# A PEER step on one core: the norms' rows loaded for each use, their memory a place for fetched rows in between

## The chip, the cores and the metric

The kernel runs on one core of a Trainium2 chip. The metric is the device time of one execution in microseconds (us). The engines are named as in the profile: PE (TensorE, matmuls; PEld its weight loads), DVE (VectorE), ACT (ScalarE), POOL (GpSimd) and SP (SyncE, which only issues DMAs here). Each runs its own instructions in the order in which the scheduler wrote them, and waits for the others by semaphores.

## The reference, cut to what matters

One decoder layer on 512 prompt tokens and 32 sample tokens: a mixer (retention heads and a causal convolution on a shared projection), a layer norm, a retrieval of experts (PEER), a second layer norm.

```python
def layer_norm(x, g, b): ...  # over 1024 features, then * g + b
...
x = layer_norm(ALPHA * x + mix, ln1_g, ln1_b)
ffn = peer(x, w_query, sub_keys_1, sub_keys_2, peer_u, peer_v)
x = layer_norm(ALPHA * x + ffn, ln2_g, ln2_b)

def peer(...):            # per token and head (8 heads)
    s1, s2 = q1 @ keys1, q2 @ keys2      # 128 scores each
    v1, i1 = top_k(s1, 16); v2, i2 = top_k(s2, 16)
    sv, ci = top_k(v1[:, None] + v2[None, :], 16)
    idx = e1 * 128 + e2                  # one of 16384 experts
    gate = softmax(sv)
    act = gelu(peer_u[idx] . x)
    out = sum(gate * act * peer_v[idx])  # 128 experts a token
```

## The kernel before

**Two ways to the experts.** For 288 of the token rows the experts are fetched. A *slot* is one expert for each of 128 partitions: an indirect DMA on POOL's queue (`gather`, L670) brings 128 rows of `uv` (a u row and a v row of 1024 numbers each, 1 MB a slot) into a *place*, a tile named `g`; DVE takes the dot of the u half with the token (L676, the *dot*), ACT the gelu and the gate (L687, L688), and DVE adds the weighted v half to the accumulator (L693, the *sum*). The place is then free. Three gathers follow one another: the first 128 prompt tokens (I, 128 slots, numbers 0 to 127), the samples (Is, 32 slots, four heads' groups side by side on the partitions), the next 128 prompt tokens (Ib, 128 slots). The other 256 tokens go the dense way: all 128 x 128 experts are scored on PE (`scores_of`, L947, one *key* of 128 experts at a time, a 512 KB load by SP), and the chosen ones are picked by one-hot products (`build`: A, M and B on DVE and ACT, L1076 on PE), whose result is multiplied into the gelus (Ga to Gd, L1092 and L1105 on DVE); then the products with the v rows (L1133).

**The stages, in the order of the program.** The front: the first 128 tokens alone up to their expert numbers I0, then the mixer for all the others (convolution, rope, retention, output product, first norm). It has its own pools, among them `gx`, one place. Then the selection of the dense tokens' experts (`retrieve`, a long row of top-16 steps on DVE), with 44 keys' scores on PE beside it (`early_keys`); a turn of the numbers and gates into columns (L986 to L1007, with transposes L995 and ACT's copies, L999 to L1003, among them e2T); the *first pass* (`first_keys`: one-hot products for 96 keys and the scores of the 52 that are left of them); and last the products with the v rows, the second pass for the last 32 keys, and the gather Ib beside them (`phases` and `fetched`).

**Places.** `gp` has three. In the front every fourth slot up to 47 (`KX`) goes to `gx`, so there are four; the front's memory then goes to other pools, and slots 48 to 127 have the three of `gp`. Samples have three up to slot 30 and then a fourth, `gx2`, when the first pass is over; Ib has four, and five from slot 60.

**The norms' rows.** `ln1` (two tiles `lng`, `lnb` of 128 x 1024, the gain and offset on every partition) is loaded on POOL's queue behind the first rope and used by `mix_norm` up to the last chunk of the front (its last norm, tile `states`). `ln2` is loaded over the same two tiles by ACT's queue, and used by `finish` and at the end.

**What sets the order.** The scheduler of the framework lays out each engine's rows by priority, in the order in which the program emits them, as soon as its own timeline lets them start. `hold(k, ins)` puts the dots from slot k on behind an instruction of the mixer on DVE; `fence` does so for the later gathers.

## Time and profile before

| | us |
|---|---|
| runs shown | 1483.18, 1489.50, 1489.53 (median 1489.5) |
| profiled execution | 1488.64 |
| its span | 1486.7 |
| first fetch issued | 118.8 |
| last dot of I / of Is / of Ib | 743 / 909 / 1458 |

A row of the table of stretches gives the stretch, its length, and for each engine the busy time and the instructions, then the granted clock of PE, the mean busy share of the 16 DMA engines and their GB/s. With one source line asked for, the busy time is that line's alone. A row of the timeline has start and duration, engine, line, operation, and in brackets the idle time before it and what ended it. A matmul of 32-bit numbers is recorded twice, so a key's scores are 16 records and a v row's products 8.

### The profile page before, as it was taken

What the parts mean: (1) busy time and instruction counts of PE and PEld (TensorE: products, weight loads), DVE (VectorE), ACT (ScalarE), POOL (GpSimd) and SP (SyncE); (2) the same over time, 40 slices, a digit from 0 to 9 for tenths busy, and PEclk for the clock granted to TensorE, in tenths of its full rate; (3) what the DMA queues carried; (4) which work ended last, traced back from release to release, by engine and by line L of the source; (5) the groups of instructions that cost most, each with busy time, mean ns of one, the idle gap of its engine ahead of it and who ended that gap; (6) DMA issues with size and microseconds to landing.
All of it is one profiled execution on the core that took longest, in us unless ns stands there. A gap on an engine that the chain in (4) does not pass through costs nothing.

```text
span 1486.7 us, 19633 instructions
## 1 busy us (share of the span) xinstructions
PE 1415.3 (95%) x6666; PEld 966.0 (65%) x6666; DVE 1168.2 (79%) x2874; ACT 498.8 (34%) x1496; POOL 426.3 (29%) x397
## 2 busy tenths in 40 slices
PE   8899889999999999989999998998999999999998
PEld 7878455568767588878877873433454666666443
DVE  5829957998759999988878999777989766666666
ACT  1424753354122222245445534113673111111110
POOL 2171213334232221333222231243333322222230
PEclk9889899999999999999999999998999999999999
DMA  9749568978987789999988996999999999999995
GB/s 347 299 171 364 203 229 310 387 290 308 356 329 300 257 335 346 346 375 345 340 309 333 343 336 231 368 424 384 359 369 392 413 402 410 413 406 409 407 409 196
DMA packets 99537, 503.63 MB, mean 339 GB/s; under 512 B 10183, under 2 KB 21191, under 8 KB 56549
## 3 DMA queue, kind: packets, MB, share of 16 engines
q0 software_dynamic: 42240, 305.12, 52.6%
q1 hardware_dynamic: 52157, 190.10, 33.8%
q10 hardware_dynamic: 5040, 7.16, 1.5%
q8 instruction: 52, 0.85, 0.2%
q14 instruction: 48, 0.39, 0.1%
HBM read 496.97 MB, written 5.80 MB: 338 GB/s over the span
## 4 chain that ended last, share of the span: by engine, by line
PE 46%; DVE 23%; DMA 17%; issue 7%; ACT 4%; POOL 2%; ACTq 0%; SPq 0%; DVEq 0%; POOLq 0%
PE pB L1133 22%; PE sp L947 13%; DMA g<-in_uv_dram,I 7%; PE mm L217 7%; DVE acc L693 6%; DVE g L676 5%; DMA g<-in_uv_dram,Ib 5%; DMA g<-in_uv_dram,Is 4%; ACT blk L283 2%; PE mm L1076 1%; PE mm L532 1%; POOL g L670 1%; DVE iu L575 1%; PE mm L899 1%; DVE B L1060 1%
## 5 line engine op out<-in xcount | busy, mean ns | idle before, releaser
L947 PE MATMUL sp<-x1T,uv 128*128 128x256 f32 x2048 | 467.7, 384 | 2.0 <-ACT Gc L1091 1.0
L693 DVE SCALAR_TENSOR_TENSOR acc<-g,wgt,acc 128x1024 f32<-128x1024 f32 x285 | 365.1, 1281 | 86.9 <-ACT wgt L688 85.3
L947 PEld LDWEIGHTS sp<-x1T,uv 128*128 128x128 f32 x2048 | 385.7, 191 | 68.6 <-issue 13.9
L676 DVE SCALAR_TENSOR_TENSOR g<-g,x 128x1024 f32<-128x1024 f32 x288 | 350.7, 1219 | 94.2 <-DMA g<-in_uv_dram,Ib 39.9
L670 POOL DMA_INDIRECT g<-in_uv_dram,I x128 | 166.4, 1300 | 438.5 <-DVE acc L693 209.0
L670 POOL DMA_INDIRECT g<-in_uv_dram,Ib x128 | 159.3, 1245 | 360.8 <-PE pB L1133 128.7
L687 ACT ACTIVATE act<-act 128x1 f32<-128x1 f32 x288 | 57.9, 202 | 591.0 <-DVE g L676 577.0
L1133 PE MATMUL pB<-uv,Ga 128*128 128x512 f32 x352 | 158.3, 596 | 0.0
L217 PE MATMUL mm<-x1T,w 128*128 128x384 f32 (+1 forms) x448 | 152.5, 498 | 0.0
L217 PEld LDWEIGHTS mm<-x1T,w 128*128 128x128 f32 x448 | 84.4, 190 | 62.9 <-issue 30.8
L1133 PE MATMUL pB<-uv,Gb 128*128 128x512 f32 x256 | 115.1, 602 | 5.8 <-DMA uv<-in_uv_dram 4.1
L1133 PEld LDWEIGHTS pB<-uv,Ga 128*128 128x128 f32 x352 | 65.7, 190 | 69.5 <-issue 66.5
L1133 PE MATMUL pB<-uv,Gd 128*128 128x512 f32 x256 | 110.0, 592 | 0.0
L1133 PEld LDWEIGHTS pB<-uv,Gb 128*128 128x128 f32 x256 | 47.5, 190 | 70.2 <-issue 52.7
L1133 PEld LDWEIGHTS pB<-uv,Gd 128*128 128x128 f32 x256 | 48.6, 190 | 60.8 <-issue 59.3
L1052 ACT ACTIVATE off<-row,e1T 128x128 bf16<-128x128 bf16 x256 | 78.7, 392 | 2.0 <-PE mm L1076 1.8
L670 POOL DMA_INDIRECT g<-in_uv_dram,Is x32 | 41.5, 1296 | 123.0 <-DVE Ga L1105 36.9
L1133 PE MATMUL pB<-uv,Gc 128*128 128x512 f32 x160 | 75.9, 620 | 0.1
L1076 PEld LDWEIGHTS <-A 128*128 128x128 f16 x1024 | 45.5, 98 | 44.7 <-issue 28.2
L1089 ACT ACTIVATE W<-sp 128x256 f32<-128x256 f32 (+26 forms) x84 | 26.7, 318 | 133.9 <-PE sp L947 109.0
L217 PE MATMUL mm<-g,w 128*128 128x160 f32 (+1 forms) x512 | 67.0, 291 | 1.1 <-ACT score L589 1.1
L1076 PE MATMUL mm<-B,A 128*128 128x96 f16 (+1 forms) x1024 | 49.5, 192 | 18.7 <-DVE Ga L1105 7.4
(309 smaller groups left out, 1613.6 us busy)
## 6 DMA issues: line engine op xcount, KB each, us to landing
uv<-in_ut_dram SPq DMA_DIRECT2D x128, 512.0 KB
uv<-in_uv_dram SPq DMA_DIRECT2D x128, 512.0 KB
w<-in_w_in_dram SPq DMA_DIRECT2D x18, 1024.0 KB
w<-in_w_query_dram SPq DMA_DIRECT2D x15, 1024.0 KB
w<-in_w_out_dram SPq DMA_DIRECT2D x7, 1024.0 KB
g<-in_uv_dram,I POOLq DMA_INDIRECT x128, 8.3
g<-in_uv_dram,Ib POOLq DMA_INDIRECT x128, 9.4
x1T<-in_xT_dram ACTq DMA_DIRECT2D x1, 1536.0 KB
```

The source lines that it names most:

```text
L217: T.matmul(p[:, :n], w[m // 2][:, k, (m % 2) * 128:(m % 2 + 1) * 128], xT[:, k, c0:c0 + n], start=(k == 0), stop=(k == 7))
L283: S.activation(rows[j * 32:j * 32 + 32, g], u_p[g * 32:g * 32 + 32, m, p0 + j:p0 + j + w], AF.Copy)
L532: last = T.matmul(banks_[q][:, s * 256:(s + 1) * 256], src[:, k, c0:c0 + C], wo[q * 2 + s][:, k0 + k, :], start=(xT is None and k0 == 4 an ...
L670: fetch = G.indirect_dma_start(out=t, out_offset=None, in_=a["uv"], in_offset=bass.IndirectOffsetOnAxis(ap=idx[:, k:k + 1], axis=0))
L676: dot = V.scalar_tensor_tensor(t[:, :D], t[:, :D], 1.0, x1, op0=OP.mult, op1=OP.mult, accum_out=act[:, 0:1])
L687: S.activation(act[:, 1:2], act[:, 0:1], AF.Gelu)
L693: V.scalar_tensor_tensor(acc, v, wgt, acc, op0=OP.mult, op1=OP.add)
L947: mm = T.matmul(sp[:, i], u[:, k], x1T[:, k, NG2:], start=(k == 0), stop=(k == 7), skip_group_check=True)
L1052: S.activation(off[:, t], row, AF.Abs, bias=e1T[:, t1 + t:t1 + t + 1])
L1076: mm = T.matmul(pt[:, t % nt], A[t % TB], B[:, q, t % TB // 2, :, t % 2], start=(q == 0), stop=(q == 1))
L1089: S.activation(W[:, :n], sp[:, :n], AF.Gelu)
L1133: return [T.matmul(pB[b][q], W[:, b * 128:(b + 1) * 128], vt[:, q * 512:(q + 1) * 512], start=False, stop=(e == NK - 1), skip_group_check= ...
```

## The change

The rows of the norms become one tile `ln` of 128 x 2048, the size of a place, in the pool `per` with one buffer (`shared`). `norm_rows` loads both halves on POOL's queue: ln1 before the first norm as before, ln1 once more before the other chunks' norms, ln2 before the first `finish`, and ln2 once more before the samples' `finish`. In between, slots of the gather take the same tile. The gather's first 40 slots (`K5`) are emitted ahead of the rest of the front, with a priority 1100 later, and have five places (three of `gp`, `gx`, `ln`); slots 40 to 47 have four as before; 48 to 55 the three of `gp`; 56 to 119 four (`gp` and `ln`); 120 to 127 three. The samples have four up to slot 25 and three up to 29. The numbers of `hold` grow by three or four.

```diff
+K5 = 40
+K4 = (56, 120)
...
+    ln = []
+
+    def shared():
+        return per.tile([128, 2 * D], F32, name="ln")
+
+    def norm_rows(which, after=None):
+
+        t = shared()
+        ln[:] = [t[:, 0:D], t[:, D:]]
+        for half, part in zip(ln, "gb"):
+            src = a[f"{which}_{part}"]
+            load = nc.gpsimd.dma_start(half, bass.AP(tensor=src.tensor, offset=src.offset, ap=[[0, 128], [1, D]]))
+            if after is not None:
+                await_(load, after)
...
-        layer_norm(x1, n, ln1[0], ln1[1], src)
+        layer_norm(x1, n, ln[0], ln[1], src)
...
-                pool = gx if k < KX and k % 4 == 3 else gp
+                pools = (gp, gp, gp, gx, per) if k < K5 else (gp, gp, gp, gx) if k < KX else (gp, gp, gp, per)
+                if KX <= k < K4[0] or k >= K4[1]:
+                    pools = (gp,)
...
-                pool = gp if k < FREE else (gp, gp, gp, gx2[0])[k % 4]
-            t = pool.tile([128, 2 * D], F32, name="g")
+                pools = (gp, gp, gp, per) if k < FREE - 4 else (gp,) if k < FREE else (gp, gp, gp, gx2[0])
+            pool = pools[k % len(pools)]
+            t = shared() if pool is per else pool.tile([128, 2 * D], F32, name="g")
...
-    ln1 = [bc_row("lng", a["ln1_g"], D, q=nc.gpsimd, after=lastq), bc_row("lnb", a["ln1_b"], D, q=nc.gpsimd, after=lastq)]
+    norm_rows("ln1", lastq)
...
     conv_s(yS, normed)
+    now = tc.cur_priority
+    tc.cur_priority = now + 1100
+    gather0 = gather(x1_0, I0, g0_gates, acc0, range(PH * TK))
+    for _ in range(K5):
+        next(gather0)
+    tc.cur_priority = now
...
-    hold(44, conv_norm(y, n))
+    hold(48, conv_norm(y, n))
...
+    norm_rows("ln1")
     gate_heads(ons[1], gT, NS)
...
-    gather0 = gather(x1_0, I0, g0_gates, acc0, range(PH * TK))
-    for _ in range(KX):
+    for _ in range(KX - K5):
         next(gather0)
...
-    ln2 = [bc_row("lng", a["ln2_g"], D), bc_row("lnb", a["ln2_b"], D)]
...
+        norm_rows("ln2")
         finish(x1_0, [acc0[:, 0:512], acc0[:, 512:]], 128, [(0, 128, o[0][0, 0:128])], room())
...
+        norm_rows("ln2")
         t = room()
```

The dots and sums that stand on DVE ahead of some rows, counted in the order:

| ahead of | before: dots, sums | now |
|---|---|---|
| the last chunk of the first tokens' numbers (I0) | 12, 8 | 13, 9 |
| the first rope of the other tokens (L230) | 24, 23 | 26, 25 |
| the last norm of the front (L514, states) | 55, 54 | 58, 57 |
| the first top-16 step of the selection | 67, 65 | 69, 68 |
| the second table of expert numbers (L992) | 107, 105 | 116, 115 |
| the first product into Ga (L1105) | 112, 110 | 119, 117 |
| the last product of the first pass into Ga | 158, 156 | 158, 156 |

The lines of the changed kernel are higher by 17 to 27 (L670, L676, L693 are now L690, L696, L713; L992 is L1017, L1005 L1030, L1105 L1130, L1092 L1117).

DVE at the turn into columns, from the second table of expert numbers (L992, tile e) to the cast of the gates (L1005, gtT), before:

```order
L992 TENSOR_SCALAR e_4242<-e_4242 128x128
L1056 TENSOR_TENSOR M<-iot,e2T 128x768
L693 SCALAR_TENSOR_TENSOR acc<-g,wgt,acc 128x1024
L1060 TENSOR_TENSOR B<-M,gtT 128x768 x2
L676 SCALAR_TENSOR_TENSOR g,act<-g,x_0_129 128x1024
L1056 TENSOR_TENSOR M<-iot,e2T 128x768
L693 SCALAR_TENSOR_TENSOR acc<-g,wgt,acc 128x1024
L676 SCALAR_TENSOR_TENSOR g,act<-g,x_0_129 128x1024
L693 SCALAR_TENSOR_TENSOR acc<-g,wgt,acc 128x1024
L676 SCALAR_TENSOR_TENSOR g,act<-g,x_0_129 128x1024
L693 SCALAR_TENSOR_TENSOR acc<-g,wgt,acc 128x1024
L1005 CAST gtT<-e_4249 128x128
```

The same place now (L1017 to L1030):

```order
L1017 TENSOR_SCALAR e_4240<-e_4240 128x128
L650 TENSOR_REDUCE Es<-oh 128x32
L696 SCALAR_TENSOR_TENSOR g,act<-g,x_0_129 128x1024
L1037 CAST Is<-Es 128x32
L713 SCALAR_TENSOR_TENSOR acc<-g,wgt,acc 128x1024
L1030 CAST gtT<-e_4247 128x128
```

Three dots and four sums stood between the two rows, and now one of each. On PE, behind the transposes of that table, two more keys' scores stood ahead of the first one-hot products, and now one.

DVE near the end of the first pass, from the first product that takes 13 keys of Gc on (Ga, Gb and Gc are the dense block's gates times gelus), before:

```order
L1105 SCALAR_TENSOR_TENSOR Gc<-mm,Gc 128x13x4
L693 SCALAR_TENSOR_TENSOR acc<-g,wgt,acc 128x1024
L1105 SCALAR_TENSOR_TENSOR Ga<-mm,Ga 128x44x4
L1092 TENSOR_TENSOR Gc<-Gc,W 128x224
L1056 TENSOR_TENSOR M<-iot,e2T 128x768
L1105 SCALAR_TENSOR_TENSOR Ga<-mm,Ga 128x44x4
L1092 TENSOR_TENSOR Gc<-Gc,W 128x228
L676 SCALAR_TENSOR_TENSOR g,act<-g,x_0_7032 128x1024
L1105 SCALAR_TENSOR_TENSOR Gb<-mm,Gb 128x32x4
L1105 SCALAR_TENSOR_TENSOR Gc<-mm,Gc 128x14x4
L1060 TENSOR_TENSOR B<-M,gtT 128x768 x2
L676 SCALAR_TENSOR_TENSOR g,act<-g,x_0_7032 128x1024
```

and now:

```order
L1130 SCALAR_TENSOR_TENSOR Gc<-mm,Gc 128x13x4
L696 SCALAR_TENSOR_TENSOR g,act<-g,x_0_7033 128x1024
L1130 SCALAR_TENSOR_TENSOR Gb<-mm,Gb 128x32x4
L1130 SCALAR_TENSOR_TENSOR Gc<-mm,Gc 128x14x4
L1085 TENSOR_TENSOR B<-M,gtT 128x768 x2
L1130 SCALAR_TENSOR_TENSOR Ga<-mm,Ga 128x44x4
L1117 TENSOR_TENSOR Gc<-Gc,W 128x228
L713 SCALAR_TENSOR_TENSOR acc<-g,wgt,acc 128x1024
L1130 SCALAR_TENSOR_TENSOR Ga<-mm,Ga 128x44x4
L1117 TENSOR_TENSOR Gc<-Gc,W 128x232
```

From that row to the last product into Ga there were six dots, two of them in these rows, and now there is one.

POOL at the second load of ln1, which is now between fetches (I is the table of slot rows; hrs is the scale of a retention chunk's head norm):

```order
L690 DMA ln<-in_uv_dram,I_133 128x2048
L690 DMA g<-in_uv_dram,I_133 128x2048 x4
L184 DMA ln<-in_ln_g_dram 128x1024
L184 DMA ln<-in_ln_b_dram 128x1024
L212 TENSOR_SCALAR hrs<-hrs 128x4
L213 TENSOR_TENSOR hrs<-hrs,mhalf 128x4
L690 DMA g<-in_uv_dram,I_133 128x2048 x4
```

The first row is slot 39, the last one in `ln`; the loads wait for its sum on DVE, and the head norm's scale and slots 44 to 47 stand behind them.

More of the change, by code (lines that the diff above doesn't have):

```diff
@@ L660, in gather @@
             if x1 is x1_0:
-                pool = gx if k < KX and k % 4 == 3 else gp
+                pools = (gp, gp, gp, gx, per) if k < K5 else (gp, gp, gp, gx) if k < KX else (gp, gp, gp, per)
+                if KX <= k < K4[0] or k >= K4[1]:
+                    pools = (gp,)
             elif late:
-                pool = (gp, gp, gp, gx2[0])[k % 4] if k < 60 else (gp, gp, gp, gx2[0], bx)[k % 5]
+                pools = (gp, gp, gp, gx2[0]) if k < 60 else (gp, gp, gp, gx2[0], bx)
             else:
-                pool = gp if k < FREE else (gp, gp, gp, gx2[0])[k % 4]
-            t = pool.tile([128, 2 * D], F32, name="g")
+                pools = (gp, gp, gp, per) if k < FREE - 4 else (gp,) if k < FREE else (gp, gp, gp, gx2[0])
+            pool = pools[k % len(pools)]
+            t = shared() if pool is per else pool.tile([128, 2 * D], F32, name="g")
             at = step(k) if late else -1
@@ L700, in finish @@
             V.scalar_tensor_tensor(t[:n, c], x1[:n, c], ALPHA, f[h][:n], op0=OP.mult, op1=OP.add)
-        layer_norm(t, n, ln2[0], ln2[1], table=table)
+        layer_norm(t, n, ln[0], ln[1], table=table)
         for p0, p1, dst in dsts:
@@ L858, in tile_step @@
     retain(2, *before(2))
-    hold(45, steps["p"])
+    hold(49, steps["p"])
     banks[:] = [ps]
@@ L880, in tile_step @@
     retain(3, *third)
-    hold(47, steps["p"])
+    hold(51, steps["p"])
     gate_heads(ons[2], gT, NS + C)
@@ L885, in tile_step @@
     mix_b(NS, C)
-    hold(49, steps["ln"])
+    hold(53, steps["ln"])
     xrs[0], pms[0] = fe.tile([128, D], F32, name="xr0"), None
@@ L893, in tile_step @@
     mix_b(NS + C, C)
-    hold(53, steps["ln"])
+    hold(56, steps["ln"])
     pq0, known = [mmps() for _ in range(4)], NS + 2 * C
@@ L904, in tile_step @@
     mix_b(NS + 2 * C, C, parts[1])
-    hold(55, steps["ln"])
+    hold(58, steps["ln"])
     for m in range(4):
@@ L1227, in tile_step @@
         t = gp.tile([128, 2 * D], F32, name="g")[:, :D]
-        layer_norm(t, 128, ln2[0], ln2[1], pB[b], True)
+        layer_norm(t, 128, ln[0], ln[1], pB[b], True)
         for q in range(2):
```

## The prediction

> **What bounds the kernel now.** I read the page first, for its span and the slices.
>
> ```profile
> span 1486.7 us, 19633 instructions
> PE 1415.3 (95%) x6666; PEld 966.0 (65%) x6666; DVE 1168.2 (79%) x2874; ACT 498.8 (34%) x1496; POOL 426.3 (29%) x397
> ...
> DVE  5829957998759999988878999777989766666666
> ...
> DMA  9749568978987789999988996999999999999995
> ```
>
> VectorE (DVE) is full only in the middle, the DMA engines from slice 25 on. The 79% and 95% average over stages with different limits, so the second view is the table of stretches, cut at the front, the prompt block's waits, the dense block's selection, its conversion to one-hot rows, the first pass over the keys, and the rest.
>
> ```profile
> core 0: us, PE busy (x) PEld busy (x) DVE busy (x) ACT busy (x) POOL busy (x), PEclk, DMA share, GB/s
> ...
> 186.00:260.00 74.00, 68.79 (x398) 39.08 (x397) 47.34 (x82) 33.32 (x81) 21.70 (x17) 0.95 0.75 270
> ...
> 372.00:453.70 81.70, 76.41 (x370) 58.02 (x363) 52.28 (x72) 15.85 (x52) 23.67 (x21) 0.96 0.89 342
> 453.70:656.00 202.30, 200.90 (x893) 161.17 (x892) 195.38 (x697) 60.03 (x169) 53.53 (x41) 1.00 0.86 320
> 656.00:665.20 9.20, 4.01 (x20) 3.29 (x19) 6.13 (x7) 2.70 (x11) 2.93 (x3) 0.94 1.01 420
> 665.20:907.60 242.40, 228.69 (x1401) 190.74 (x1401) 213.60 (x468) 111.91 (x447) 63.20 (x50) 0.97 0.89 330
> 907.60:1034.00 126.40, 119.15 (x316) 50.33 (x315) 96.13 (x252) 28.24 (x77) 43.40 (x29) 0.98 0.93 373
> 1034.00:1486.70 452.70, 444.96 (x1711) 248.48 (x1710) 328.10 (x585) 120.50 (x382) 118.36 (x101) 0.99 0.95 379
> ```
>
> VectorE idles 26.7 us of 186 to 260 and 29.4 us of 372 to 453.7, but 6.9 us of the selection (453.7 to 656), which it bounds. In the first pass (665.2 to 907.6) it idles 28.8 us and TensorE (PE) 13.7, so both bound it. Third, the chain that ended last, for the end:
>
> ```profile
> 1352.30 3.45 PE sp L947 x16
> 1355.76 3.43 PE pB L1133 x8
> ...
> 1369.55 109.88 PE pB L1133 x256
> ```
>
> From 1034 TensorE runs without a gap, 3.45 us for a key's scores and 3.43 for its products. Nothing that changes among the fetches shortens that. A gain must come from an earlier end of the first pass, at about 907.
>
> **The places.** What a slot of the gather takes:
>
> ```profile
> POOL g L670 <- DVE acc L693: 256.0, 78, 16.3
> ...
> L670 POOL DMA_INDIRECT g<-in_uv_dram,I x128 | 166.4, 1300 | 438.5 <-DVE acc L693 209.0 <-DVE iu L575 40.4 <-DVE cand L576 15.9
> ...
> g<-in_uv_dram,I POOLq DMA_INDIRECT x128, 8.3
> ...
> 453.70:656.00 202.30, 50.12 (x82) 1.00 0.86 320
> ...
> 453.70:656.00 202.30, 52.25 (x41) 1.00 0.86 320
> ```
>
> GpSimd (POOL) waits 256 us in all for a sum that frees a place. A slot takes 1.3 us of issue, 8.3 to landing, a dot of 50.12 / 41 = 1.22 us and a sum of 52.25 / 41 = 1.27 (the last two rows: the dots' line, with its accumulator reads, and the sums' line): about 12 us with nothing in between, so 4 us a slot with three places and 3 with four. The selection did 41 slots in 202.3 us, 4.9 each: the places were often, but not always, what was short. A slot costs VectorE 2.5 us wherever it stands.
>
> **The change, part by part.** The counts are those of the order shown with the change.
>
> *The front.* The order puts 2 dots and 3 sums more ahead of the selection (69/68 for 67/65): 2 x 1.22 + 3 x 1.27 = 6.3 us, which the 26.7 and 29.4 us of idle hide. Were that cover gone, it would cost 6.3. The two reloads of ln1 stand on POOL behind the sum of slot 39 and ahead of a head norm's power and six fetches.
>
> ```profile
> L166 POOL DMA_DIRECT2D lng<-in_ln_g_dram x1 | 0.6, 602 | 21.0 <-ACT ropeB L228 21.0
> ```
>
> That is 2 x 0.6 us behind a sum which the norm's own scaling follows directly. I take +1 us; between -3 (dots that wait less) and +8 (one landing in the open). The norm that needs the rows is ten slots later, so their landing is covered.
>
> *The selection.* Seven slots more come ahead of the second table of expert numbers (L992: 107/105 less 67/65, now 116/115 less 69/68): 7 x 2.5 = 17.5 us more of VectorE. Half of its 6.9 us of idle should go, so +14; bounds 10.6 and 17.5. Behind L992 stand the rows that decide when the first one-hot product starts:
>
> ```profile
> 656.10 1.28 DVE L693 SCALAR_TENSOR_TENSOR acc<-g,wgt,acc 128x1024 f32<-128x1024 f32 x1
> 659.16 1.23 DVE L676 SCALAR_TENSOR_TENSOR g<-g,x 128x1024 f32<-128x1024 f32 x1 [1.77 <-DMA g<-in_uv_dram,I]
> ...
> 660.99 1.28 DVE L693 SCALAR_TENSOR_TENSOR acc<-g,wgt,acc 128x1024 f32<-128x1024 f32 x1 [0.60 <-ACT wgt L688]
> 662.20 1.22 DVE L676 SCALAR_TENSOR_TENSOR g<-g,x 128x1024 f32<-128x1024 f32 x1
> ...
> 652.93 7.07 PE L947 MATMUL sp<-x1T,uv 128*128 128x256 f32 x32
> 665.19 1.44 PE L1076 MATMUL mm<-B,A 128*128 128x96 f16 x16 [5.19 <-ACT e2T L1003]
> ```
>
> TensorE waits 5.19 us for e2T, which ScalarE (ACT) evacuates behind three slots' gelus, and those wait for dots that wait for fetches. Now one dot stands there for three. Two slots and the waits in them go: 2 x 2.5 + 1.77 + 2 x 0.60 = 8.0 us. So the first product moves from 665.2 by 14 - 8 to about 671: **+6** (bounds 0 and +13). TensorE arrives 3.45 us earlier, since one key now comes behind the first products, so it waits 5.2 + 6 + 3.45 = 14.6 us there.
>
> *Its clock.*
>
> ```profile
> 659.50:664.10 4.60, 0.50 (x3) 0.20 (x2) 3.40 (x6) 1.11 (x5) 1.55 (x1) 1.00 1.02 426
> 664.10:671.00 6.90, 5.81 (x27) 4.91 (x27) 5.88 (x10) 3.73 (x15) 2.24 (x3) 0.51 0.97 403
> 671.00:678.00 7.00, 7.00 (x56) 6.63 (x55) 6.01 (x13) 3.77 (x16) 3.09 (x3) 1.00 0.77 266
> ```
>
> After the wait the granted clock is 0.51 for 6.9 us, a loss of 3.4 us. I take the same loss after the longer wait, so nothing is added. If it grew with the wait, 3.4 x 14.6 / 5.2 = 9.5, the sum would lose 6 us and give 1484.7. The Trainium skill, "TensorE: Matmul & The Clock Gate", section "What's actually happening", has two states and a release after about 3.4 us of sustained work, whatever the idle time was; by it nothing is added. The trace agrees in the level and in the end at full clock, while its 6.9 us are two such windows; no run here shows a longer wait at this place.
>
> *The first pass.* 42 dots are left behind L992 for 51, of which about 8 fall behind the first product: 8 x 2.5 = **20 us** less for VectorE, if its 28.8 us of idle stay. TensorE sets the other bound:
>
> ```profile
> 881.69 3.52 PE sp L947 x16
> ...
> 905.62 0.33 DVE L1105 SCALAR_TENSOR_TENSOR Ga<-mm,Ga 128x176 f32<-128x176 f32 x1
> ...
> L1076 PE MATMUL mm<-B,A 128*128 128x96 f16 x512 | 32.5, 208 | 12.7 <-DVE Ga L1105 7.4 <-ACT e2T L1003 5.2
> ```
>
> The pass has 220 us from its first product to the end of the last key's scores (885.2; in the chain) and 20.4 more to its last Ga. With 53 keys for 52 and half of the 7.4 us of waits for Ga gone, the 220 stay: + 3.45 - 3.7. In the 20.4 the order had six dots behind the first product with 13 keys of Gc and now has one, so 5 x 2.5 = 12.5 us go, and with 1 or 2 us of the waits for fetches between them **14**. I take the middle, **-17**; bounds -8, where half of that tail stays, and -25, where VectorE's waits for fetches go as well.
>
> *The rest.* From there the order has the same rows, so all shifts alike: 0, bounds +-3. The ln2 reloads are 2 MB and the ln1 reload 1 MB, against 1 MB that leaves the ACT queue: 2 MB more, about 5 us at 420 GB/s, spread over stretches with a share of 0.86 to 0.89, so hidden. Uncovered they would cost those 5.
>
> **The sum**, against the profiled execution's own 1488.64 us: +1 + 6 - 17 + 0 = -10, so **1478.6 us**. The runs shown have a median of 1489.5 and a lowest of 1483.2.
>
> **Rivals.**
>
> *The gain is swallowed* (0.29). The selection takes its seven slots at the full 17.5 us and the first product slips by 10 or more, while the first pass shortens by 8 to 13: 1485 to 1490. For it: VectorE is 97% busy in the selection (195.38 of 202.30), so a slot placed there is work moved to another bound stage. Against it: the two slots behind L992.
>
> *The change does not do what it says* (0.05). The order has only 2 slots more at the front's end, for a place of its own over 40 slots. If DVE holds them up in the selection as well, the time is 1488 +- 3.
>
> *The loads of the keys starve* (0.10): slower. Four fetches under way instead of three take DMA time from the 512 KB that each key's scores need, in 453.7 to 665.2, where TensorE has no slack. It is seen later, where products and fetches run together:
>
> ```profile
> PEld pB L1133 <- DMA uv<-in_uv_dram: 20.0, 24, 2.6
> ...
> 453.70:665.20 211.50, 150.93 (x688) 129.31 (x686) 1.00 0.87 325
> ```
>
> That is 24 waits of 0.83 us. The second row is the scores' line: 688 records, 43 keys. Late on half of them, the loads cost 21 x 0.83 = 18 us: 1478.6 + 18 = 1497. From 12 late keys on (10 / 0.83) the change is a loss. It decides where the DMA share reaches 1. Against it: 7 slots are 7 MB more in 202 us, 35 GB/s on 320, a share of about 0.95; and from 1034 the scores run at 3.45 us with fetches beside them. The Trainium skill, "DMA: Bandwidth & Descriptors", section "Queues, rings and completion order", has each DMA engine go round its queues a packet at a time; by that a longer POOL queue takes no larger share, and this loss would be 0. The waits above show that the loads can be late all the same.
>
> *More than the sum* (0.06). The gather's waits in the front (372 to 453.7) shorten the norms that follow them, and the first pass loses all its waits: 1462 to 1467.
>
> **How the numbers follow.** The forecast has 0.50. Its own range, with its terms' bounds taken together, is 1469 to 1484. To hold 8 in 10 the range takes in the swallowed case and half of the starved one: **1466 to 1492**. A measurement of this kernel can tell about 0.5% (7.4 us) from no change. Faster by more, so below 1481.2: 0.42 of the forecast's 0.50 and the upside, 0.48. Slower by more: the starved loads, 0.10. Within it: 0.42, the rest of the forecast (0.08), the swallowed case and the one without effect.
>
> **What would show it.** Right: the first one-hot product at 668 to 675, with a wait of 10 to 17 us of TensorE before it; the last Ga product of the first pass at 892 to 898 for 905.6; fetch waits on DVE acc below 256 us. In the swallowed case the last Ga stands past 900. Starved loads show as waits of sp L947 for DMA uv before 665, with TensorE's rows there past 3.45 us a key. The sum is wrong if the start of the selection (453.7) moves by more than 8 us, which the reordered front could do, or if the stretch behind 907 does not shift as a whole.

## The result, and the profile after

The changed kernel takes 1469.8 us (median of 6 runs, 1465.6 to 1473.5), the kernel before 1485.7 beside it (6 runs, 1483.2 to 1489.5): 15.9 us less, a ratio of 0.989 with a 95% interval of 0.987 to 0.991. In a later comparison it was 1468.4 for 1486.8, ratio 0.988 [0.985, 0.991]. The direction was forecast, the size was not: the forecast of 1478.6 us was 10 us below the profiled execution of before and 7 below the median of 1485.7. The profiled execution took 1470.17 us, against 1488.64 before; this pair is 18.5 us apart, 2.6 more than the medians, so the lengths of the stages below carry some 2 us of chance.

The page of the changed kernel, with rows that answer to those shown of before:

```profile
span 1468.4 us, 19660 instructions
...
PE 1402.6 (96%) x6666; PEld 961.0 (65%) x6666; DVE 1166.0 (79%) x2874; ACT 501.2 (34%) x1498; POOL 421.3 (29%) x403
```

VectorE's busy time is within 2.2 us of before (1168.2). TensorE's recorded time is 12.7 us shorter for the same 6666 instructions; its mean granted clock rose only from 0.977 to 0.979, which is worth about 3 us of the span, so most of that difference is not explained by the clock. The table of stretches of the changed kernel, cut at the same events (the last three cuts are the start of the selection, the first one-hot product and the last Ga of the first pass):

```profile
core 0: us, PE busy (x) PEld busy (x) DVE busy (x) ACT busy (x) POOL busy (x), PEclk, DMA share, GB/s
186.00:260.00 74.00, 74.00 (x424) 43.22 (x424) 56.44 (x86) 38.67 (x95) 23.79 (x21) 0.98 0.91 339
372.00:447.20 75.20, 73.39 (x369) 55.32 (x362) 50.70 (x69) 15.71 (x52) 26.09 (x23) 1.00 0.91 361
447.20:664.00 216.80, 204.73 (x894) 163.50 (x893) 212.71 (x721) 66.00 (x186) 61.00 (x48) 0.98 0.90 337
664.00:885.50 221.50, 221.16 (x1414) 189.69 (x1413) 194.15 (x442) 106.67 (x427) 52.66 (x45) 1.00 0.88 331
```

The same stretch of the kernel before, to its last Ga, with TensorE's and VectorE's busy time in second and fourth place:

```profile
665.20:906.00 240.80, 227.09 (x1397) 190.07 (x1397) 212.00 (x464) 110.34 (x441) 63.20 (x50) 0.97 0.89 330
```

In the first pass TensorE idled 240.8 - 227.1 = 13.7 us before and 0.3 after, and its clock went from 0.97 to 1.00. The stages, with the forecast beside them (us from the start of the span in the first two columns):

| | before | after | length changed by | forecast |
|---|---|---|---|---|
| start of the selection | 453.7 | 447.2 | -6.5 | +1 |
| first one-hot product | 665.2 | 664.0 | +5.3 | +6 |
| last Ga of the first pass | 906.0 | 885.5 | -19.3 | -17 |
| end of the span | 1486.7 | 1468.4 | +2.2 | 0 |

Three terms are within 2.3 us. The front is off by 7.5 of the 8.3 us that the sum is off. TensorE's idle time in the first pass is 13.4 of its 19.3 us; the other 5.9 are busy time, though one key's scores more stand in the pass.

### The profile page after: what moved, and what is told of

It reads as the page before. It is cut to its first block, busy times and chain, and to the rows that moved or that the text cites. A ratio compares the mean times of both kernels' runs of the same rounds, so it can differ in the third digit from the quotient of the medians.

```text
span 1468.4 us, 19660 instructions
## 1 busy us (share of the span) xinstructions
PE 1402.6 (96%) x6666; PEld 961.0 (65%) x6666; DVE 1166.0 (79%) x2874; ACT 501.2 (34%) x1498; POOL 421.3 (29%) x403
## 4 chain that ended last, share of the span: by engine, by line
PE 49%; DVE 26%; DMA 12%; issue 7%; ACT 4%; POOL 2%; SPq 0%; DVEq 0%; POOLq 0%; ACTq 0%
PE pB L1158 20%; PE sp L972 18%; DVE acc L713 6%; PE mm L234 6%; DMA g<-in_uv_dram,Ib 5%; DVE g L696 5%; DMA g<-in_uv_dram,I 3%; DMA ln<-in_uv_dram,I 2%; PE mm L1101 2%; POOL g L690 1%; PE mm L549 1%; DVE ln L696 1%; DVE iu L592 1%; DVE iu L595 1%; DMA uv<-in_ut_dram 1%
## 5 line engine op out<-in xcount | busy, mean ns | idle before, releaser
L713 DVE SCALAR_TENSOR_TENSOR acc<-g,wgt,acc 128x1024 f32<-128x1024 f32 x255 | 326.3, 1279 | 68.4 <-ACT wgt L708 67.5
L696 DVE SCALAR_TENSOR_TENSOR g<-g,x 128x1024 f32<-128x1024 f32 x258 | 314.0, 1219 | 61.2 <-DMA g<-in_uv_dram,Ib 45.8
L690 POOL DMA_INDIRECT g<-in_uv_dram,Ib x128 | 161.7, 1263 | 359.6 <-PE pB L1158 134.8
L690 POOL DMA_INDIRECT g<-in_uv_dram,I x104 | 128.3, 1233 | 322.1 <-DVE acc L713 197.4
L1114 ACT ACTIVATE W<-sp 128x256 f32<-128x256 f32 (+26 forms) x84 | 26.7, 317 | 136.4 <-PE sp L972 126.1
L234 PEld LDWEIGHTS mm<-g,w 128*128 128x128 f32 x512 | 65.8, 195 | 1.0 <-ACT score L606 1.0
L690 POOL DMA_INDIRECT g<-in_uv_dram,Is x26 | 32.5, 1248 | 116.3 <-DVE Ga L1130 29.6
```

What stands on the lines that cost most here:

```text
L234: T.matmul(p[:, :n], w[m // 2][:, k, (m % 2) * 128:(m % 2 + 1) * 128], xT[:, k, c0:c0 + n], start=(k == 0), stop=(k == 7))
L690: fetch = G.indirect_dma_start(out=t, out_offset=None, in_=a["uv"], in_offset=bass.IndirectOffsetOnAxis(ap=idx[:, k:k + 1], axis=0))
L696: dot = V.scalar_tensor_tensor(t[:, :D], t[:, :D], 1.0, x1, op0=OP.mult, op1=OP.mult, accum_out=act[:, 0:1])
L713: V.scalar_tensor_tensor(acc, v, wgt, acc, op0=OP.mult, op1=OP.add)
L1114: S.activation(W[:, :n], sp[:, :n], AF.Gelu)
```

## Experiments

Ratios are to the kernel before in the same comparison, 5 rounds each, medians in us. The first stage is counted from one early row of TensorE (the L555 row near 95 us, L572 in the changed kernel), not from the span's start: ahead of that row, two profiles of one program differ by 2 us (see the last section). Behind it, too, single profiles scatter: e4 and e6 are edited behind the front alone, and their fronts are 355.5 and 350.8 us for the changed kernel's 352.8. So a difference of 3 us between two fronts counts only where the rows show its cause. The early row (TensorE's timeline), before and then changed:

```profile
95.11 1.11 PE L555 MATMUL mm<-cst,x 128*128 128x128 f32 x4 [3.61 <-DVE x L514]
```

```profile
94.38 1.12 PE L572 MATMUL mm<-cst,x 128*128 128x128 f32 x4 [3.57 <-DVE x L531]
```

"Dots" are the gather's dots in the first pass, "PE idle" TensorE's idle time there.

| kernel | median | ratio [95%] | front | selection | first pass | dots | PE idle | rest |
|---|---|---|---|---|---|---|---|---|
| before | 1485.7 | 1 | 358.6 | 211.5 | 240.8 | 48 | 13.7 | 580.7 |
| changed | 1469.8 | 0.989 [0.987, 0.991] | 352.8 | 216.8 | 221.5 | 41 | 0.3 | 582.9 |
| changed, again (e11) | 1468.4 | 0.988 [0.985, 0.991] | 353.0 | 215.7 | 222.6 | 41 | 1.1 | 581.0 |
| e1 | 1491.9 | 1.004 [1.002, 1.006] | 355.6 | 207.7 | 245.2 | 50 | 16.6 | 586.4 |
| e2 | 1479.6 | 0.994 [0.992, 0.996] | 354.8 | 211.6 | 239.0 | 48 | 13.4 | 579.4 |
| e3 | 1484.3 | 0.998 [0.996, 0.999] | 359.6 | 212.7 | 234.1 | 43 | 5.4 | 584.1 |
| e4 | 1474.5 | 0.991 [0.988, 0.993] | 355.5 | 210.2 | 232.2 | 46 | 11.4 | 583.0 |
| e5 | 1474.5 | 0.992 [0.989, 0.995] | 358.8 | 213.3 | 223.6 | 42 | 0.8 | 579.0 |
| e14 (e5 again) | 1474.4 | 0.993 [0.991, 0.995] | 359.6 | 213.1 | 223.6 | 42 | 0.8 | 580.8 |
| e13 | 1470.4 | 0.991 [0.989, 0.993] | 356.3 | 213.1 | 223.6 | 42 | 0.8 | 580.1 |
| e8 | 1478.6 | 0.996 [0.994, 0.998] | 352.0 | 212.6 | 234.5 | 43 | 5.4 | 584.5 |
| e10 | 1468.3 | 0.988 [0.985, 0.991] | 351.7 | 217.8 | 221.5 | 41 | 0.3 | 580.9 |
| e6 | 1469.0 | 0.989 [0.986, 0.992] | 350.8 | 213.0 | 227.2 | 44 | 6.4 | 582.3 |
| e7 | 1465.9 | 0.987 [0.984, 0.991] | 353.8 | 214.9 | 218.1 | 41 | 0.4 | 582.0 |
| e12 | 1471.9 | 0.990 [0.986, 0.993] | 353.6 | 210.4 | 225.8 | 44 | 4.9 | 583.3 |
| e9 | 1471.2 | 0.989 [0.986, 0.992] | 353.1 | 211.5 | 222.8 | 45 | 3.2 | 586.4 |

### Two suspects for the front

The first is a wait that the prediction had passed over. The kernel before, timeline of TensorE around 412 us:

```profile
408.17 1.04 PE L555 MATMUL mm<-cst,states 128*128 128x128 f32 x8
412.45 3.79 PE L899 MATMUL mm<-x1T,blk 128*128 128x128 f32 x16 [3.25 <-ACT x1T L558]
```

ACT's timeline of the same kernel, ahead of that:

```profile
407.18 0.20 ACT L687 ACTIVATE act<-act 128x1 f32<-128x1 f32 x1 [6.58 <-DVE g L676]
...
411.39 0.20 ACT L687 ACTIVATE act<-act 128x1 f32<-128x1 f32 x1 [3.68 <-DVE g L676]
...
411.82 1.06 ACT L558 ACTIVATE x1T<-mm 128x512 f32<-128x512 f32 x2
```

TensorE had finished the last transposes at 409.2. ACT copied them out at 411.8, behind the gelus of slots whose dots waited for fetched rows. The products then ran at half clock for 6.9 us, as the table of stretches of that kernel shows:

```profile
411.50:418.40 6.90, 5.95 (x28) 5.95 (x29) 3.66 (x4) 1.85 (x6) 1.62 (x2) 0.51 0.96 336
```

That is 3.25 us of wait and about 3 of clock. In the changed kernel the copy stands ahead of those gelus, and TensorE waits 0.25 us (ACT's timeline, then TensorE's):

```profile
408.09 1.08 ACT L575 ACTIVATE x1T<-mm 128x512 f32<-128x512 f32 x2 [7.83 <-PE mm L572]
411.15 0.20 ACT L707 ACTIVATE act<-act 128x1 f32<-128x1 f32 x1 [1.98 <-DVE ln L696]
```

```profile
407.45 1.04 PE L572 MATMUL mm<-cst,states 128*128 128x128 f32 x8
408.74 2.05 PE L926 MATMUL mm<-x1T,blk 128*128 128x128 f32 x16 [0.25 <-ACT x1T L575]
```

**e1** makes this one difference in the kernel before:

```diff
-            S.activation(x1T[:, q * 4:q * 4 + 4, c0:c0 + n], pt[:, :, :n], AF.Copy)
+            steps["x1T"] = S.activation(x1T[:, q * 4:q * 4 + 4, c0:c0 + n], pt[:, :, :n], AF.Copy)
...
-            S.activation(act[:, 1:2], act[:, 0:1], AF.Gelu)
+            gelu = S.activation(act[:, 1:2], act[:, 0:1], AF.Gelu)
+            if x1 is x1_0 and k >= 55:
+                behind(gelu, steps["x1T"])
```

> The kernel before, with one change of order: on ACT the gelus of the fetched rows from slot 55 on stand behind the last copy of the last chunk's x1T, which before stood behind the gelus of slots 55 to 57 and, through them, behind fetched rows that had not landed (PE waited 3.25 us for that copy at 412.5 us and then ran 6.8 us at half clock). Theory 1 (the front's 6.5 us are this wait and the half clock behind it): the wait at 412 goes, the selection starts at 446.5 to 449 us of the span instead of 453.7, and the total is 4 to 7 us below the kernel before. Theory 2 (the front's gain comes from ACT's 13.5 us stand at its DMA for the samples' rows, 206.5 to 220 us): the selection starts at 453 to 455 us and the total is within 2 us of before.

The wait went (the timeline of TensorE in e1, its last transposes, its last products of x1T, and a later row):

```profile
408.56 1.04 PE L555 MATMUL mm<-cst,states 128*128 128x128 f32 x8
409.85 2.05 PE L901 MATMUL mm<-x1T,blk 128*128 128x128 f32 x16 [0.25 <-ACT x1T L558]
...
672.10 2.08 PE L519 MATMUL pB<-scaled,x1T 128*128 128x128 f32 x8 [4.94 <-ACT Ga L981]
```

From the last transposes (408.56) to the selection (448.3) e1 takes 39.7 us; the kernel before takes 45.5 (408.17 to 453.7) and the changed kernel 39.8 (407.45 to 447.2). That is the whole 5.8 us that theory 1 wanted. But e1 reaches the last transposes 2.8 us later, counted from the early row (its first products of x1T, at 391.25, took 5.84 us for the 4.15 of before), so its front is only 3.0 us shorter, and the total is 0.4% **longer**. The slots that were held back came due in the first pass: 50 dots for 48, TensorE idle 16.6 us for 13.7, with a new wait of 4.94 us at 672. That these slots are what made the total longer is argued from the counts, not shown by a run. A copy that stands ahead only pays if the slots behind it are not lost.

The second suspect is a stand of ACT, a time in which it does nothing, at a DMA that it issues itself. The kernel before, ACT's timeline:

```profile
206.15 0.33 ACT L453 ACTIVATE on<-samples 128x16 f32<-128x16 f32 x2 [0.54 <-POOL on L449]
219.59 0.35 ACTq L888 DMA_DIRECT2D xr<-in_x_dram  x1
219.99 0.20 ACT L687 ACTIVATE act<-act 128x1 f32<-128x1 f32 x1 [13.51 <-issue]
```

The load overwrites xr, which SP's timeline writes out first:

```profile
206.54 0.38 SPq L469 DMA_DIRECT2D out_dram<-xr  x1
```

ACT issued the load only 13 us after that write was issued, and did nothing in between; "issue" says only that no semaphore explains the wait. VectorE's sum waited 7.8 us behind it (220.6) and TensorE 5.07 (223.6). That the load waits for the write can be read from the packets in the traces: the last packet of that write ends at 219.07 us, and the load is issued at 219.59. In e1, e3, e5 and e14, which have the stand too, the load follows the last packet by 0.37 to 0.42 us.

The write is slow there because fetches move beside it. In the kernel before POOL had waited 16.26 us for a place, and four fetches went out from 204.10 to 210.82; the write's packets (512 KB) start at 209.62 and need 9.45 us. In the changed kernel, with a fifth place, a fetch goes out at 192.43 and the next only at 207.81; SP issues the write at 204.72, and its packets move from 205.64 to 208.34, in 2.7 us. e4 and e11, which have the fifth place too, show the same gap between fetches; e3, e5 and e14, which have four places, show the four fetches. POOL's timeline, before and then changed:

```profile
204.10 1.69 POOL L670 DMA_INDIRECT g<-in_uv_dram,I  x1 [16.26 <-DVE acc L693]
```

```profile
192.43 1.68 POOL L690 DMA_INDIRECT ln<-in_uv_dram,I  x1 [3.93 <-DVE acc L713]
...
207.81 1.68 POOL L690 DMA_INDIRECT g<-in_uv_dram,I  x1 [3.20 <-DVE acc L713]
```

So the write is done when ACT reaches the load, and there is no stand (ACT's timeline, changed):

```profile
209.92 0.36 ACTq L915 DMA_DIRECT2D xr<-in_x_dram  x1
211.12 0.30 ACT L708 ACTIVATE wgt<-act,GT 128x1 f32<-128x1 f32 x1 [1.05 <-DVE acc L713]
```

**e2** is the kernel before with that load on SP's queue:

```diff
-    nc.scalar.dma_start(xrs[0][:NS], a["x"][128:128 + NS])
+    nc.sync.dma_start(xrs[0][:NS], a["x"][128:128 + NS])
```

> The kernel before, with the load of the samples' rows (the last use of xr in the front) issued on SP's queue and not on ACT's, so that ACT no longer stands 13.5 us at 206.5 us behind the write that the load waits for. Theory 2 (the front's gain comes from this stand): rope's first VectorE instruction at 257 us instead of 262.5, the selection starts at 446 to 449 us, total 4 to 7 us below before. Theory 1 (it comes from the copies of x1T at 412 us): the first part of the front is shorter by some 5 us, but the selection starts at 452 to 455 us and the total is within 2 us of before. If SP, which issues in order, is itself held by the write, the front gets longer by up to 8 us, and the run tells nothing on theory 2.

The stand is gone: in ACT's timeline the gelu of that place starts at 212, behind its dot.

```profile
212.03 0.20 ACT L687 ACTIVATE act<-act 128x1 f32<-128x1 f32 x1 [5.93 <-DVE g L676]
```

The front is 3.8 us shorter, and the gain is kept to the end: 7.3 us in the median. In the profiles 1.8 us more lie in the first pass, 1.3 in the rest and 0.7 ahead of the early row, each no more than a stage moves between two profiles of one kernel. SP now stands in ACT's place (it issues the write at 206.17 and the load at 215.93); its next row, a write, still goes out earlier than before, at 216.71 for 223.93. That the stand costs time holds for this kernel, while theory 2's claim on the front's gain is taken up below; the wait for x1T is still there at 408 (3.55 us).

### The parts of the change

**e3** has only the fourth place behind the front; **e4** only the front's part. Against the changed kernel, e3:

```diff
-                pools = (gp, gp, gp, gx, per) if k < K5 else (gp, gp, gp, gx) if k < KX else (gp, gp, gp, per)
+                pools = (gp, gp, gp, gx) if k < KX else (gp, gp, gp, per)
...
-    tc.cur_priority = now + 1100
...
-    norm_rows("ln1")
     gate_heads(ons[1], gT, NS)
```

(the holds and the place of the emission are as in the kernel before), and e4:

```diff
-                if KX <= k < K4[0] or k >= K4[1]:
+                if k >= KX:
...
-                pools = (gp, gp, gp, per) if k < FREE - 4 else (gp,) if k < FREE else (gp, gp, gp, gx2[0])
+                pools = (gp,) if k < FREE else (gp, gp, gp, gx2[0])
```

> The changed kernel without its part in the front: the fourth place serves slots 56 to 119 and the samples' first slots, but the front has four places, the gather is emitted where it was, and the rows of the first norm are loaded once. If the prediction's sum was right in its terms behind the front and wrong in the front alone: the selection starts at 452.5 to 455 us as before, its length to the first one-hot product is 213 to 220 us (before 211.5, changed 216.8), from there to the last score of the first pass 219 to 228 us (before 240.4, changed 221.2), total 10 to 15 us below before. If the gain behind the front needs the slots that the front has already taken: first pass 230 us or more, total 2 to 6 us below before.

> The changed kernel without its part behind the front: fifth place, early emission, and the first norm's rows loaded twice stay; from slot 48 on three places as before, the samples three places for their first 30 slots, and the second norm's rows loaded once. If the two parts add up: the selection starts at 446 to 449 us (before 453.7), its length and that of the first pass are as before (210 to 214 and 238 to 242 us), total 4 to 8 us below before. If the front's gain is lost again at the next wait for fetched rows: the selection starts at 447 us but is 215 us or longer, total within 3 us of before.

The fourth place alone brings 2.5 us, the front's part alone 12.4; together 14.9, near the 15.9 of both. So the larger part goes with the front's edit, where the prediction saw none. Only 3.1 of e4's 12.4 us are in the front itself: its first pass has 46 dots for 48 and is 8.6 us shorter, against the case that it would stay as before. 2.4 of these 8.6 us are TensorE's idle time, and 6.2 its busy time (220.85 us for 227.09), at a clock of 0.99 for 0.97. e3 came out as the second case said: its first pass is 6.7 us shorter with 43 dots, but its front stays (359.6) and its rest is 3.4 longer.

**e5** is the changed kernel with four places in the front and one load of ln1, but with the early emission and the later holds.

```diff
-                pools = (gp, gp, gp, gx, per) if k < K5 else (gp, gp, gp, gx) if k < KX else (gp, gp, gp, per)
+                pools = (gp, gp, gp, gx) if k < KX else (gp, gp, gp, per)
...
-    norm_rows("ln1")
     gate_heads(ons[1], gT, NS)
```

> The changed kernel without the fifth place in the front and without the second load of the first norm's rows: the first 48 slots rotate over four places as before, while the early emission, the later holds and the fourth place behind the front stay. If the front's gain comes from the fifth place (through ACT's load of the samples' rows and SP's loads, which stand in the order as before in this kernel, so that ACT's stand of some 13 us returns): the selection starts at 452 to 455 us, total near that of the fourth place alone, 2 to 6 us below before. If it comes from the early emission and the later holds: the selection starts at 446 to 449 us and the total is 12 to 18 us below before.

Its front is that of before (358.8), and ACT's stand is back, as its timeline shows:

```profile
219.33 0.20 ACT L707 ACTIVATE act<-act 128x1 f32<-128x1 f32 x1 [13.32 <-issue]
```

So the front's gain comes with the fifth place (and the second load of ln1 that goes with it). That the wait for x1T goes is not enough for it: it is all but gone here too, with 0.88 us at 414.69. The total is 10.4 us below before, between the two cases: its first pass is nearly as good as that of the changed kernel. In e3 it is 10.5 us longer: it has one dot and about one key's scores more there (1431 records of TensorE for 1416), and TensorE idles 5.4 us for 0.8. Which of early emission and later holds does that was not taken apart.

### The stand and the fifth place

**e8** is e3 with e2's edit. **e10** is the changed kernel with e2's edit. **e9** was to put the stand back into the changed kernel: the write of xr behind a later write on SP, and a gelu behind the load on ACT:

```diff
+            if b == 6:
+                second = write
+            else:
+                done = write()
+            if b == 2:
+                behind(second(), done)
...
+    behind(gelus[12], nc.scalar.dma_start(xrs[0][:NS], a["x"][128:128 + NS]))
```

> The fourth place behind the front alone (front as before), and the load of the samples' rows on SP's queue instead of ACT's. If the two gains add (measured apart: -2.5 and -7.3 us against before): 8 to 12 us below before, selection at 446 to 449 us. If the fifth place does more than take ACT's stand away: at least 4 us short of the changed kernel's -16. If they do not add: 2 to 7 us below before.

> The changed kernel with the load of the samples' rows on SP's queue. In the kernel before this edit alone took 7.3 us away. Theory (the changed kernel has already lost that stand): 0, so 1466 to 1473, selection at 445 to 448 us. Rival (the load still holds ACT up, 4.83 us at 216.2 us, and this is part of the path): selection 3 to 5 us earlier, total 1462 to 1467.

> The changed kernel with ACT's stand at its load of the samples' rows put back: on SP the write of xr that the load waits for stands behind the first write of the other states (219.3 us in the changed kernel, for 204.7), and on ACT the gelu of the thirteenth slot stands behind the load, so that ACT stands from about 207 to 225 us. Theory (ACT's stand is what made the front of before longer): the convolution norm at 294.8 us comes 5 us or more later, the selection starts at 451 to 462 us for 447.2, total 1474 to 1486. Rival (the stand is hidden, the front's gain comes from the fifth place's earlier slots): selection within 2 us of the changed kernel's, total 1466 to 1473.

In e8 the front falls from 359.6 to 352.0, and the other stages stay as in e3, within 0.5 us. The median is 6.3 us below before, where e3's was 2.5 in another comparison. That is less than the 8 to 12 us expected if the two gains add, but e8's interval runs from 3.7 to 8.9 us, so whether they add is open. In e10 nothing changes: 1468.3 beside 1468.4 for the changed kernel in the same comparison, front 351.7 for 353.0. In the changed kernel there was no stand left to take. e9 was to take 1474 to 1486 us and took 1471.2; it says nothing on the stand, since the scheduler put other copies ahead of the load, and ACT was busy until it (ACT's timeline in e9), so that the load went out at 224.46 without a stand:

```profile
218.84 6.10 ACT L300 ACTIVATE blk<-u_p 32x412 f32<-32x412 f32 x11
224.46 0.35 ACTq L921 DMA_DIRECT2D xr<-in_x_dram  x1
```

**e13** therefore takes the stand away where there is one: e5 with e2's edit, beside e5 again (**e14**).

> The changed kernel without the fifth place in the front and without the second load of the first norm's rows, and with the load of the samples' rows on SP's queue. Beside it runs the same kernel with that load on ACT, where ACT stood 13.3 us. Theory (what the fifth place does in the front is to take that stand away, by the order that it gives to SP and ACT): the selection starts 4 to 7 us earlier than in the kernel beside it, counted from the same early row of TensorE, and the total is 1466 to 1471, that of the changed kernel. Rival (the fifth place is worth its own slots): the selection starts within 2 us of the kernel beside it, total 1473 to 1477.

> The changed kernel without the fifth place and the second load of the first norm's rows, again: 1471 to 1478 as before, ACT's stand of 13 us at the load of the samples' rows, the selection's start within 2 us of 453.8 us of the span, counted from the same early row of TensorE.

e14 has the stand (its timeline of ACT):

```profile
215.62 0.20 ACT L707 ACTIVATE act<-act 128x1 f32<-128x1 f32 x1 [11.80 <-issue]
```

e13, in the same view, has not:

```profile
212.39 0.20 ACT L707 ACTIVATE act<-act 128x1 f32<-128x1 f32 x1 [5.98 <-DVE g L696]
```

The front is 3.3 us shorter, between the two cases, and the median 3.9 us lower, at 1470.4, within what the theory wanted; the two intervals overlap, so the total alone would not decide. With e2 (3.8) and e8 (7.6) the stand is worth 3 to 8 us of the front. e13's front (356.3) is still 3.5 us longer than the changed kernel's, so by these profiles the stand is about half of what the fifth place brings there; what the other half is stays open.

### The changed kernel again, and can it be beaten?

> The changed kernel again, beside the other three on one chip: 1466 to 1473, and the selection's start within 2 us of 447.2. It says by how much a stage moves between two profiles of one kernel.

e11 is the changed kernel unedited; its stages moved by at most 1.9 us. Two waits are left in the changed kernel. TensorE's timeline, the rotated keys and then the turn into columns:

```profile
293.83 0.49 PE L411 MATMUL mm<-blk 128*128 128x128 f32 x2 [3.50 <-DVE blk L251]
...
626.97 0.33 PE L1020 MATMUL mm<-cst,e 128*128 128x128 f32 x1 [2.00 <-DVE e L1014]
...
633.02 0.47 PE L1020 MATMUL mm<-cst,e 128*128 128x128 f32 x1 [5.72 <-DVE e L1017]
...
658.59 0.33 PE L1020 MATMUL mm<-cst,e 128*128 128x128 f32 x1 [2.98 <-DVE e L1017]
```

**e7** moves three dots behind the rotation and the convolution norm, **e6** holds the dots from slot 108 on behind the second table, **e12** does both:

```diff
-            V.tensor_sub(y[:, m, :n], y[:, m, :n], pm[:, :n])
+            steps["sub"] = V.tensor_sub(y[:, m, :n], y[:, m, :n], pm[:, :n])
...
+    for d in dots[34:]:
+        behind(d, steps["sub"])
...
-        V.tensor_scalar(e2, e2, 1.0 / NK, None, op0=OP.mult)
+        hold(108, V.tensor_scalar(e2, e2, 1.0 / NK, None, op0=OP.mult))
```

> The changed kernel, with the dots of slots 34 to 36 held behind the convolution norm's subtractions, which follow the last rotated key, so that TensorE's wait of 3.50 us for it at 293.8 us, and the 6.8 us at half clock behind it, should go. Theory (the changed front gained 5.4 us up to the rotation and lost 4.7 of them again at this wait): the wait falls below 1 us, the last row of x1T's products (416.2 us) and the start of the selection (447.2) come 3 to 6 us earlier, total 1463 to 1468. Rival (the three dots come due again before the chunks' norms, which wait in their place): the selection starts at 446 to 449 us and the total is 1468 to 1474.

> The changed kernel, with the dots of slots from 108 on held behind the second table of expert numbers, so that 104 dots stand ahead of it and not 112. Theory (a dot ahead of the table lengthens the selection by 2.4 us, a dot behind it the first pass): the second table comes at some 640 us for 658, the waits of 10.7 us of TensorE at the transposes go, the first one-hot product starts 8 to 16 us earlier than in the changed kernel (648 to 656), and the first pass takes 8 x 2.4 = 19 us more of VectorE; total within 4 us of the changed kernel (1466 to 1474). If TensorE's waits and half clock there were a loss of their own: 1460 to 1466. If the first pass pays more than the selection gains: 1475 or more.

> Both candidates together: the dots of slots 34 to 36 behind the convolution norm's subtractions, and the dots from slot 108 on behind the second table of expert numbers. If their effects add (measured apart: -3.9 and -0.8 us against the changed kernel, each within its noise): 1462 to 1467. If a slot pushed out of one stage costs as much in the next: 1467 to 1473. Slower than 1473 if the first pass pays for both.

In e7 the wait at 293.8 is gone and the rotation ends earlier, but a wait of 5.61 us stands later in its place (TensorE's timeline in e7):

```profile
377.56 2.93 PE L549 MATMUL mm<-w,blk 128*128 128x256 f32 x6 [5.61 <-DVE blk L397]
```

The front is 353.8 for 352.8, as the rival said; the median of 1465.9 lies in the theory's range. e6 shortens the selection by 3.8 us, and pays 5.7 in the first pass: there are three dots more there, where eight were meant, and TensorE idles 6.4 us again. e12 came out as if a slot pushed out of one stage costs as much in the next. None of e6, e7 and e12 can be told from the changed kernel: 1469.0, 1465.9 and 1471.9 with intervals that overlap its own.

## Why the prediction was right in three terms and wrong in one

**The front (forecast +1, measured -6.5; -5.8 from the early row): the step that failed.** I costed it as VectorE's work alone, "2 dots and 3 sums more ahead of the selection ... which the 26.7 and 29.4 us of idle hide", with -3 as the best case. The dots were hidden as said. What I left out is that the change also shifts the rows of POOL, ACT and SP against one another, and that TensorE's waits in the front hang on these. I named the reordered front as what could spoil the sum, and gave it no term.

The last transposes divide the front. Counted from the early row they come at 313.1 us in the kernel before (408.17 less 95.11) and at 313.1 in the changed kernel (407.45 less 94.38); from there to the selection it is 45.5 and 39.8 us. So the net gain of 5.8 us stands behind the last transposes. It is ACT's copy of x1T, which no longer stands behind gelus: the wait of 3.25 us and the half clock behind it went, and e1, which makes this one change of order, has the same 39.7.

The copy alone is not the front's gain, for e3, e5 and e14 have it too (40.2, 41.0 and 39.5 us) and a front as long as before. They reach the last transposes only at 317.8 to 320.1 us, with ACT's stand, and e13, which takes the stand out of e5, at 314.4. So against e5 and e14 the fifth place shortens the stretch ahead of them by 4.8 and 7.0 us: it moves the fetches away from the write, and ACT's stand goes. The stand's own gain does not show in the sum. At the sums of the convolution norm (300.75 in the kernel before, 296.18 in the changed one) the changed kernel is 3.8 us ahead, counted from the early row; at the first products of x1T (392.55 and 391.83) it is level again, with the wait at 293.8 and a granted clock of 0.50 from 294.4 to 301.2 between. When that wait is moved, one at 377.6 takes its place (e7). Why the scheduler sets the copy ahead of the gelus, and what else the fifth place does ahead of the last transposes, stays open. I saw the idle time of that stretch in the table of stretches and did not ask what had ended it; ACT's row of 13.51 us and TensorE's of 3.25 answer that.

**The selection (+6, measured +5.3).** Right in mechanism and size. The second table comes 13.2 us later counted from the selection's start, where 14 was forecast. The waits of 14.6 us came as 10.7 us in three pieces, at the transposes and not at the first product. I assumed the loss of clock to be that of before, 3.4 us, however long the wait. The two stretches at half clock in the changed kernel:

```profile
628.80:635.60 6.80, 2.58 (x7) 2.17 (x8) 6.80 (x27) 2.08 (x4) 2.53 (x3) 0.51 0.86 286
659.50:663.00 3.50, 3.50 (x10) 2.74 (x9) 2.54 (x7) 1.65 (x7) 0.75 (x2) 0.52 1.01 415
```

TensorE was busy 6.1 us of them, so about 3 us were lost. The 9.5 us of the other reading did not come. The loss changed its stage, though: in the kernel before, the half clock behind the wait lay in the first pass (664.1 to 671.0, in the prediction's rows), and now it lies in the selection, whose clock goes from 1.00 to 0.98. So the two sizes fit in part because the same loss is counted in another stage.

**The first pass (-17, measured -19.3).** Right in direction and nearly in size, and in part by luck: the sum took the clock's loss as unchanged, while the clock of this pass went from 0.97 to 1.00. VectorE's busy time falls from 212.0 to 194.2 (forecast -20), and its idle time stays: 28.8 before, 27.4 after. Of TensorE's waits not a part but all went. TensorE's idle time goes with the number of dots in the table: with 50 dots in the pass it idles 16.6 us, with 48 13.4 to 13.7, with 46 11.4, with 44 4.9 to 6.4, with 43 5.4, with 42 0.8 (e9 alone stands apart, with 45 and 3.2). From there on TensorE bounds the pass (221.16 us busy of 221.50), so that fewer dots should bring nothing and the bound of -25 was out of reach; no run has fewer than 41.

**The rest (0, measured +2.2).** Within the 3 us given. VectorE builds B later: 6.50 us of wait for 3.46 at the start of the second pass. In e11 that wait is 5.66 and the rest 581.0 us, so part of the 2.2 is chance.

**The checks.** The first product came 4.0 us and the last Ga 6.5 us ahead of the ranges named; with the front's 6.5 us added both lie in them. The start of the selection moved by less than the 8 us that were to show the sum wrong, and yet it was this term that failed, so that sign was set too wide. "Fetch waits on DVE acc below 256" was a poor check. The changed kernel's waits of POOL:

```profile
POOL g L690 <- DVE acc L713: 250.9, 80, 27.6
...
POOL ln L690 <- DVE acc L713: 62.6, 18, 12.1
```

Together they are 313.5 us: with more places fetches are issued earlier and wait longer for a place, while the kernel is faster.

**The rivals.** The starved loads are refuted: no wait of sp for DMA uv stands ahead of 664, at a DMA share of 0.90. The change without effect is refuted by the 15.9 us. The swallowed gain is refuted: the selection lost 5.3 us, the first pass gained 19.3. "More than the sum", at 1462 to 1467, named the two places where more came, waits in the front and all waits of the first pass; it had 0.06.

## What to carry to other kernels

An edit that adds buffers can also reorder every engine that serves them, so read the waits of the engine that sets the end (here TensorE) one by one, follow each to what ended it, and ask whether the new order still has it; idle time in a table of stretches is the place to begin, not an allowance. A DMA issued from a computing engine's queue, whose target must first be written out, holds up all that stands behind it there: ACT stood 11.8 to 13.9 us where the write moved beside fetches, and not at all where it moved alone. Taking it to a queue that computes nothing was worth 7.3 us in the kernel before and nothing in the changed one. Work moved out of a stage pays until that stage's other engine is full; here TensorE idled 1.1 us or less in the first pass with 42 dots or fewer.

## What the runs showed of the hardware

The clock's drops do not repeat exactly. The changed kernel's two profiles had mean clocks of 0.74 and 0.91 in the stretch from 60 to 80, around a wait of some 3 us (2.83 and 3.03). In the first the clock was 0.50 already from 66 to 70, ahead of the wait, and in the second 1.00. The table of stretches of the first profile:

```profile
60.00:80.00 20.00, 15.39 (x71) 12.84 (x70) 9.34 (x38) 9.60 (x24) 8.07 (x18) 0.74 0.64 250
```

and of the second (e11):

```profile
60.00:80.00 20.00, 15.16 (x76) 12.24 (x74) 9.89 (x38) 9.45 (x25) 8.84 (x20) 0.91 0.61 239
```

The early row was 1.7 us earlier in the second (92.66 us for 94.38), and the start of the selection 1.6. A shift of 2 us between single profiles is therefore not to be read as an effect of an edit, until it is counted from a row behind such a drop.

The same write of 512 KB needed 2.7 us from its first to its last packet where no fetch moved beside it (the changed kernel), and 9.45 us beside four fetches of 1 MB (the kernel before).
